# A gated delta rule's recurrence: one inverse product per block behind keys times state, instead of a second solve ahead of it

## The chip, the cores and the metric

The kernel runs on one core of a Trainium2 chip. The metric is the device time of one execution in microseconds; before the change it is 1047.45 us, the median of three runs (1047.32 to 1048.46).

## The reference

One layer of a hybrid block on 512 tokens of width 1024: a half-step SwiGLU feed-forward network, a token mixer, and a second feed-forward network, each behind an adaptive norm. The mixer has two groups of four heads: a gated delta rule (GDN) and latent attention (MLA). Only the delta rule's chunk recurrence is touched. With G the running sum of the log decays in a chunk, the reference computes per head and chunk:

```python
A = where(strict, beta[:, None] * (k @ k.T) * decay, 0)
M = A + eye(CHUNK)
rhs = concatenate([v * beta[:, None], k * (beta * exp(G))[:, None]], axis=-1)
u, wk = split(triangular_solve(M, rhs, lower=True, unit_diagonal=True))
# scan over chunks, state S of 128 x 128 per head:
v_new = u - wk @ S
o     = (q * exp(G)[:, None]) @ S + ((q @ k.T) * decay) @ v_new
S     = S * exp(G[-1]) + (k * exp(G[-1] - G)[:, None]).T @ v_new
```

Afterwards o is normalised per head, multiplied by a gate, and goes with the attention output through the output projection. Everything is float32.

## The kernel before

**Tiling.** Tokens are handled as four blocks p of 128 (the kernel's chunk for the recurrence), heads as four groups of 128 columns in a 128 x 512 tile. Dense products split both operands into a high and a low part and use three matmuls for each 128 x 128 weight tile (lines 267 to 269, `mm3`); the delta rule's own products are plain float32 matmuls of 128 x 128, which the trace shows as two matmul records each (x8 for the four heads).

**Order of the work.** The program is a set of Python generators that emit instructions; a `Side` holds generators and `step(n)` advances them n yields. A planner then orders each engine's queue by emission order among what it expects to be ready. In the mixer three sides matter: `chain` (the keys' norms, the matrix A, its blockwise inverse, the join of the inverse's 64-wide halves at lines 1639 to 1654, then the solves), `deltas` (queries, values), and `att` (attention). They are stepped between the dense products of the input projection. When those are done, a `while` loop at line 2066 steps them on; once attention is finished, `fill` holds `out_attended`: the attention half of the output projection, 32 steps of three 128 x 512 matmuls, each fourth followed by an update of xT on VectorE (line 2121), each eighth preceded by a weight load with its split (wh on ScalarE, line 193; wl on VectorE, line 198).

**The solves** (`solve`, line 1667): for each block, U (the transposed block inverse) times the scaled values gives u (line 1685), copied from PSUM by ScalarE; for blocks 1 to 3, decayed keys (kbg, a VectorE multiply at line 1678) times U gives w (line 1694), copied by ScalarE. The keys for the state update (kd) are scaled on VectorE as well (line 1681). Multiplies go through a helper and show as line 1232.

**The recurrence** (`recur`, line 1698), between lines 2080 and 2107: inside `matmuls_in_order` TensorE's instructions keep the order of emission, apart from those that are emitted by `loosely`. Each block yields twice. Before the first yield: w times S (line 1711), vn = u − that (VectorE, line 1713), S times its decay on GpSimd, q times S (line 1719) and its scaled copy (ScalarE, line 1721). After it: kd times vn (line 1726), the new S, qk times vn (line 1734), o. At each yield the loop puts in three steps of `fill` and two of `gated`. Block 0 has no state and needs no w.

**The gated output** (`gated_out`, line 1742) of a block is opened behind the block: square on ScalarE (hn, line 1772), sum (gs, line 1773) and ve (line 1748) on VectorE, a power on GpSimd (ry, line 179), a scaling on VectorE (on); then, at the next block's first yield and behind that yield's fill steps, four transposes on TensorE (line 1757) and the products with the gate (mf, mh, ml). They are in the kept order, not loose. After block 3 come `fill.step(4)` and the rest of the gated outputs, then the delta half of the output projection in two token halves (`out_half`), whose first half lies in `fill` as well.

**Buffers.** 128 x 512 tiles come from a pool of 56 (`slots`), some from a second pool of 12 (`late`); among the latter are all convolution outputs (`conv`, line 1431) and the gate z.

Of the kernel before, what the change touches and what calls it, by code (L numbers as in the profile page):

```python
# [14 lines left out]
AF = mybir.ActivationFunctionType  # L15
ALU = mybir.AluOpType
AX = mybir.AxisListType

P = 128
# [3 lines left out]
NB = NT // P  # L23
# [56 lines left out]
class Block:  # L80
# [1347 lines left out]
        self.table(d, d, AF.Exp)  # L1428
        return d

    def conv(self, p, ct):

        nc = self.nc
        a = self.slot(s="cv", late=True)
        wj = lambda j: self.cwT[:, 12 * j + ct:12 * j + ct + 1]
        nc.scalar.activation(a, p, AF.Copy, scale=wj(3))
        for d in range(1, 4):
            nc.vector.scalar_tensor_tensor(out=a[:, d:], in0=p[:, :NT - d], scalar=wj(3 - d), in1=a[:, d:], op0=ALU.mult,  # L1438
                                           op1=ALU.add)
        return a  # L1440
# [217 lines left out]
    def values(self, vT):  # L1658

        h4 = lambda x: x.rearrange("p (h d) -> p h d", h=4)  # L1660
        self.vb = []
        for p in range(NB):
            self.vb.append(self.slot(s="vb"))
            self.mul(h4(self.vb[p]), h4(self.token_major(vT, p)), self.bc(self.kn[:, 4 * p:4 * p + 4], 4))
            yield

    def solve(self, p):

        nc = self.nc
        h4 = lambda x: x.rearrange("p (h d) -> p h d", h=4)  # L1670
        hs = lambda h: slice(h * P, (h + 1) * P)
        c4 = slice(4 * p, 4 * p + 4)
        u = self.inv[p]
        vb = self.vb[p]
        kt = self.kt[p]
        if p > 0:
            kbg = self.slot(s="kbg")
            self.mul(h4(kbg), h4(kt), self.bc(self.eG[:, c4], 4))
        if p < NB - 1:
            self.kd[p] = self.slot(s="kd")  # L1680
            self.mul(h4(self.kd[p]), h4(kt), self.bc(self.kcd[:, c4], 4))
        yield
        pu = self.aux()
        for h in range(4):
            nc.tensor.matmul(pu[:, hs(h)], u[:, hs(h)], vb[:, hs(h)], start=True, stop=True)
        self.us[p] = self.slot(s="uu")
        nc.scalar.copy(self.us[p], pu)
        yield
        if p == 0:
            self.wk[p] = True  # L1690
            return
        pw = self.aux()
        for h in range(4):
            nc.tensor.matmul(pw[:, hs(h)], kbg[:, hs(h)], u[:, hs(h)], start=True, stop=True)
        self.wk[p] = self.slot(s="w")
        nc.scalar.copy(self.wk[p], pw)

    def recur(self, p):

        nc = self.nc  # L1700
        h4 = lambda x: x.rearrange("p (h d) -> p h d", h=4)
        hs = lambda h: slice(h * P, (h + 1) * P)
        S, last = self.S, p == NB - 1
        ts = slice(p * P, (p + 1) * P)
        o = self.slot(s="o")
        if S is None:
            vn = self.us[p]
        else:
            pw = self.aux()
            for h in range(4):  # L1710
                nc.tensor.matmul(pw[:, hs(h)], self.wk[p][:, hs(h)], S[:, hs(h)], start=True, stop=True)
            vn = self.slot(s="vn")
            nc.vector.tensor_tensor(out=vn, in0=self.us[p], in1=pw, op=ALU.subtract)
            if not last:
                sg = self.slot(s="Sg")
                self.mul(h4(sg), h4(S), self.bc(self.gl[:, 4 * p:4 * p + 4], 4), nc.gpsimd)
            pq = self.aux()
            for h in range(4):
                nc.tensor.matmul(pq[:, hs(h)], self.qT[h][:, ts], S[:, hs(h)], start=True, stop=True)
            for h in range(4):  # L1720
                nc.scalar.activation(o[:, hs(h)], pq[:, hs(h)], AF.Copy, scale=self.eG[:, 4 * p + h:4 * p + h + 1])
        yield
        if not last:
            pst = self.aux()
            for h in range(4):
                nc.tensor.matmul(pst[:, hs(h)], self.kd[p][:, hs(h)], vn[:, hs(h)], start=True, stop=True)
            self.S = self.slot(s="S")
            if S is None:
                nc.vector.tensor_copy(self.S, pst)
            else:  # L1730
                nc.vector.tensor_tensor(out=self.S, in0=sg, in1=pst, op=ALU.add)
        po = self.aux()
        for h in range(4):
            nc.tensor.matmul(po[:, hs(h)], self.qk[p][:, hs(h)], vn[:, hs(h)], start=True, stop=True)
        if S is None:
            nc.scalar.copy(o, po)
        else:
            nc.vector.tensor_tensor(out=o, in0=o, in1=po, op=ALU.add)
        self.o[p] = o
        yield  # L1740
# [238 lines left out]
    def mixer(self, nb):  # L1979
        nc, tc = self.nc, self.tc  # L1980
# [13 lines left out]

        def conv_done(ct0, dst):
            def f(i, p):
                dst.append(self.conv(p, ct0 + i))
            return f

        def silu(tiles):  # L2000
# [1 line left out]
                self.table(t, t, AF.Silu)  # L2002

        self.inv, self.ready64 = [None] * NB, [None] * NB
        self.kd, self.us, self.o, self.wk = ([None] * NB for _ in range(4))
        self.S = None

        def prepared():
# [31 lines left out]
        silu(vT)  # L2040
        deltas.add(self.values(vT))

        def solving():
            solves = Side(wide=2)
            solves.add(*(self.solve(p) for p in range(NB)))
            while solves.open or solves.todo:
                solves.step(2)
                yield

        chain.add(solving())  # L2050
# [12 lines left out]

        rest = Side(wide=3)
        rest.add(others())
        while self.wk[1] is None or deltas.open or deltas.todo:
            chain.step(2)
            deltas.step()
            rest.step(4)
            if not rest.open and not rest.todo:  # L2070
                fill.step(1)

        def loosely(side, n):
            with self.traced() as block:
                side.step(n)
            self.loose.update(i.name for i in block)
# [103 lines left out]
```

## Time and profile before

| what | value |
| --- | --- |
| median of three runs | 1047.45 us (1047.32 to 1048.46) |
| the profiled execution's own time | 1047.25 us |
| its span, first to last instruction | 1045.6 us |
| TensorE busy | 1029.0 us, 98% |
| VectorE busy | 682.6 us, 65% |
| ScalarE busy | 448.6 us, 43% |
| GpSimd busy | 48.2 us, 5% |
| granted TensorE clock | 0.999 |
| first solve (line 1685) starts | 626.1 us |
| last product of the recurrence (line 1734) starts | 661.1 us |

Times of instructions are from the span's start. A row of the timeline merges neighbours of one line: its start, its length, engine, line, operation, output and inputs by the program's names, shapes and count; a bracket at the end gives the idle time of the engine ahead of it and what ended it. Lengths on TensorE are modelled to the end of the pipeline, so neighbouring rows overlap, and the cost of a group in a stream is read from start to start.

### The profile page before, as it was taken

To read this page: it belongs to the slowest core of one execution; us is meant where nothing else is said; L and a number is where in the kernel's file an instruction comes from. 1 tells how busy PE (TensorE), PEld (TensorE's weight loads), DVE (VectorE), ACT (ScalarE), POOL (GpSimd) and SP (SyncE) were. 2 spreads that over 40 slices of the span, in tenths; PEclk is the share of its full clock that TensorE was granted. 3 is DMA by queue.
4 is the path that set the end of the run, shared out by engine and by line. 5 is a ranking of instruction groups with operands and counts; after the bars stand their busy time and mean duration, and the time that the engine had idled before them with its cause. 6 is when DMAs were issued, how large, how long until landed. Compare 5 with 4: busy or idle time off the path is not lost.

```text
span 1045.6 us, 16109 instructions
## 1 busy us (share of the span) xinstructions
PE 1029.0 (98%) x6379; PEld 882.2 (84%) x6379; DVE 682.6 (65%) x1251; ACT 448.6 (43%) x781; POOL 48.2 (5%) x113
## 2 busy tenths in 40 slices
PE   6999999999999999999999999999999999999998
PEld 4778878788887799888778779998999999999986
DVE  4488984333486636648878556788778778777633
ACT  4343222232222226749565464465345444344422
POOL 1000000000000011100010111310000000000000
PEclk9999999999999999999999999999999999999999
DMA  9989973323586439712212201173423334333222
GB/s 274 292 232 322 298 218 101 100 84 94 190 285 220 155 102 231 185 40 54 69 41 56 72 22 41 41 162 101 141 81 102 104 99 121 91 92 109 74 61 81
DMA packets 203689, 136.88 MB, mean 131 GB/s; under 512 B 13777, under 2 KB 186590, under 8 KB 203614
## 3 DMA queue, kind: packets, MB, share of 16 engines
q1 hardware_dynamic: 202318, 131.14, 42.6%
q0 software_dynamic: 1296, 4.72, 2.4%
q8 instruction: 50, 0.82, 0.3%
q14 instruction: 25, 0.20, 0.1%
HBM read 128.63 MB, written 2.49 MB: 125 GB/s over the span
## 4 chain that ended last, share of the span: by engine, by line
PE 90%; ACT 4%; DVE 4%; issue 1%; DMA 1%; POOL 0%; SPq 0%; POOLq 0%; ACTq 0%; DVEq 0%
PE pa L267 20%; PE pa L268 20%; PE pa L269 20%; PE pb L872 6%; PE pb L873 6%; PE pb L874 6%; PE pb L267 1%; PE pb L268 1%; PE pb L269 1%; PE pb L1909 1%; PE pb L418 1%; PE pb L1939 1%; PE pb L1494 1%; DVE cv L1438 1%; PE pb L1912 1%
## 5 line engine op out<-in xcount | busy, mean ns | idle before, releaser
L267 PE MATMUL pa<-hh,wh 128*128 128x512 f32 (+1 forms) x565 | 216.8, 384 | 0.4 <-ACT hh L465 0.4
L193 ACT CAST wh<-wr 128x1024 fp32r<-128x1024 f32 (+1 forms) x106 | 107.9, 1018 | 250.6 <-PE pa L268 177.8
L268 PE MATMUL pa<-hl,wh 128*128 128x512 f32 (+1 forms) x565 | 214.7, 380 | 0.5 <-DVE hl L457 0.3
L269 PE MATMUL pa<-hh,wl 128*128 128x512 f32 (+1 forms) x565 | 214.5, 380 | 0.0
L198 DVE TENSOR_TENSOR wl<-wr,wh 128x1024 fp32r<-128x1024 f32 (+1 forms) x97 | 114.2, 1178 | 104.0 <-ACT wh L193 101.6
L267 PE MATMUL pa<-ah,wh 128*128 128x512 f32 (+1 forms) x396 | 145.5, 368 | 0.6 <-DVE xT L899 0.4
L268 PE MATMUL pa<-al,wh 128*128 128x512 f32 (+1 forms) x396 | 144.5, 365 | 0.0
L269 PE MATMUL pa<-ah,wl 128*128 128x512 f32 (+1 forms) x396 | 143.5, 362 | 0.0
L267 PEld LDWEIGHTS pa<-hh,wh 128*128 128x128 f32 x565 | 106.4, 188 | 23.9 <-issue 3.3
L269 PEld LDWEIGHTS pa<-hh,wl 128*128 128x128 f32 x565 | 106.3, 188 | 20.6 <-issue 0.9
L268 PEld LDWEIGHTS pa<-hl,wh 128*128 128x128 f32 x565 | 106.5, 188 | 19.6 <-DVE hl L457 1.1
L269 PEld LDWEIGHTS pa<-ah,wl 128*128 128x128 f32 x396 | 74.8, 189 | 12.0
L267 PEld LDWEIGHTS pa<-ah,wh 128*128 128x128 f32 x396 | 75.2, 190 | 10.3 <-ACT wh L193 1.7
L268 PEld LDWEIGHTS pa<-al,wh 128*128 128x128 f32 x396 | 75.2, 190 | 7.2
L577 DVE SCALAR_TENSOR_TENSOR aa<-ar,sc,aa 128x512 f32<-128x512 f32 x98 | 72.9, 747 | 8.2 <-DMA ar<-in_w_ada 6.8
L872 PE MATMUL pb<-fh,wh 128*128 128x256 f32 x144 | 40.7, 283 | 0.0
L874 PE MATMUL pb<-fh,wl 128*128 128x256 f32 x144 | 40.7, 283 | 0.0
L874 PE MATMUL pb<-hh,wl 128*128 128x256 f32 x144 | 40.7, 283 | 0.0
L873 PE MATMUL pb<-fl,wh 128*128 128x256 f32 x144 | 40.7, 282 | 0.0
L873 PE MATMUL pb<-hl,wh 128*128 128x256 f32 x144 | 40.7, 282 | 0.0
L899 DVE SCALAR_TENSOR_TENSOR xT<-pa,mod,xT 128x512 f32<-128x512 f32 (+1 forms) x40 | 29.3, 735 | 17.3 <-PE pa L269 17.3
L872 PE MATMUL pb<-hh,wh 128*128 128x256 f32 x144 | 40.6, 282 | 0.0
(445 smaller groups left out, 2003.1 us busy)
## 6 DMA issues: line engine op xcount, KB each, us to landing
wr<-in_ffn_w_in SPq DMA_DIRECT2D x82, 512.0 KB, 3.9
ar<-in_w_ada SPq DMA_DIRECT2D x48, 512.0 KB, 6.1
wr<-in_ffn_w_out SPq DMA_DIRECT2D x34, 512.0 KB, 3.9
ar<-in_w_ada SPq DMA_DIRECT2D x48, 256.0 KB, 4.8
wr<-in_w_in SPq DMA_DIRECT2D x21, 512.0 KB, 4.3
wr<-in_ffn_w_out SPq DMA_DIRECT2D x17, 384.0 KB, 3.4
wl<-wr POOLq DMA_DIRECT2D x9, 512.0 KB, 6.1
wr<-in_w_out SPq DMA_DIRECT2D x8, 512.0 KB, 3.8
```

The source lines that it names most:

```text
L193: self.nc.scalar.copy(hi, raw)
L198: self.nc.vector.tensor_tensor(out=lo, in0=raw, in1=hi.bitcast(F32), op=ALU.subtract)
L267: mm(out, wh, xh, start=start, stop=False)
L268: mm(out, wh, xl, start=False, stop=False)
L269: mm(out, wl, xh, start=False, stop=stop)
L418: nc.tensor.matmul(pg[32 * q:32 * q + 32, :256], self.sc[:, kc:kc + 1].to_broadcast([P, 32]), a[:, kc], start=(e == 0), stop=(e == 1), til ...
L577: nc.vector.scalar_tensor_tensor(out=acc, in0=a, scalar=sc, in1=acc, op0=ALU.mult, op1=ALU.add)
L872: mm(out, wh, xh, start=start and k == 0, stop=False, **kw)
L873: mm(out, wh, xl, start=False, stop=False, **kw)
L874: mm(out, wl, xh, start=False, stop=stop and k == 3, **kw)
L899: nc.vector.scalar_tensor_tensor(out=self.xT[t][:, ts], in0=p[:, ts], scalar=gate[:, t:t + 1], in1=self.xT[t][:, ts], op0=ALU.mult, op1=AL ...
L1438: nc.vector.scalar_tensor_tensor(out=a[:, d:], in0=p[:, :NT - d], scalar=wj(3 - d), in1=a[:, d:], op0=ALU.mult, op1=ALU.add)
```

## The change

The second solve is left out by using linearity: with U the inverse, u − w S equals U applied to (scaled v − decayed (k S)). Per block, the keys themselves are multiplied with the state; VectorE forms r = exp(G) · (k S) − scaled v in four instructions of 128 columns; U times r is then one product, and ScalarE's copy with scale −1 gives vn. So `solve` is now called inside `recur`, behind a yield of its own; a block has three yields, with 1, 3 and 2 fill steps instead of 3 and 3 (block 0: two yields, 1 and 3). kbg, its multiply, its product and the copy of w are gone. kd's multiply overwrites the keys in place and is emitted with the values. As the transposed keys live to the last block, their convolution output comes from `slots`, not from `late`. The main loop ends when the first inverse exists, not when the solves of the first two blocks are emitted; the remaining steps of the join are then emitted loosely inside the recurrence.

```diff
-    def conv(self, p, ct):
+    def conv(self, p, ct, late=True):
...
-        a = self.slot(s="cv", late=True)
+        a = self.slot(s="cv", late=late)
...
             self.mul(h4(self.vb[p]), h4(self.token_major(vT, p)), self.bc(self.kn[:, 4 * p:4 * p + 4], 4))
+            if p < NB - 1:
+                self.mul(h4(self.kt[p]), h4(self.kt[p]), self.bc(self.kcd[:, 4 * p:4 * p + 4], 4))
             yield
...
-    def solve(self, p):
...
-        pw = self.aux()
-        for h in range(4):
-            nc.tensor.matmul(pw[:, hs(h)], kbg[:, hs(h)], u[:, hs(h)], start=True, stop=True)
-        self.wk[p] = self.slot(s="w")
-        nc.scalar.copy(self.wk[p], pw)
+    def solve(self, p, rhs, scale):
+        u = self.inv[p]
+        pu, vn = self.aux(), self.slot(s="vn")
+        for h in range(4):
+            hs = slice(h * P, (h + 1) * P)
+            nc.tensor.matmul(pu[:, hs], u[:, hs], rhs[:, hs], start=True, stop=True)
+        nc.scalar.activation(vn, pu, AF.Copy, scale=scale)
+        return vn
...
         if S is None:
-            vn = self.us[p]
+            vn = self.solve(p, self.vb[p], 1.0)
         else:
-            pw = self.aux()
+            eg = lambda h: self.eG[:, 4 * p + h:4 * p + h + 1]
+            pk, r = self.aux(), self.slot(s="r")
             for h in range(4):
-                nc.tensor.matmul(pw[:, hs(h)], self.wk[p][:, hs(h)], S[:, hs(h)], start=True, stop=True)
-            vn = self.slot(s="vn")
-            nc.vector.tensor_tensor(out=vn, in0=self.us[p], in1=pw, op=ALU.subtract)
+                nc.tensor.matmul(pk[:, hs(h)], kT[h][:, ts], S[:, hs(h)], start=True, stop=True)
+            for h in range(4):
+                nc.vector.scalar_tensor_tensor(out=r[:, hs(h)], in0=pk[:, hs(h)], scalar=eg(h), in1=self.vb[p][:, hs(h)],
+                                               op0=ALU.mult, op1=ALU.subtract)
...
+            yield
+            vn = self.solve(p, r, -1.0)
         yield
...
-        while self.wk[1] is None or deltas.open or deltas.todo:
+        while self.inv[0] is None or deltas.open or deltas.todo:
...
-                while self.wk[p] is None:
+                while self.inv[p] is None:
                     loosely(chain, 1)
-                for _ in self.recur(p):
+                for i, _ in enumerate(self.recur(p, kT)):
                     loosely(chain, 2)
                     loosely(rest, 4)
                     if not rest.open and not rest.todo:
-                        fill.step(3)
+                        fill.step((1, 3, 2)[i])
                     gated.step(2)
```

More of the change, by code (lines that the diff above doesn't have):

```diff
@@ L1664, in values, with recur @@
             self.mul(h4(self.vb[p]), h4(self.token_major(vT, p)), self.bc(self.kn[:, 4 * p:4 * p + 4], 4))
+            if p < NB - 1:
+                self.mul(h4(self.kt[p]), h4(self.kt[p]), self.bc(self.kcd[:, 4 * p:4 * p + 4], 4))
             yield
-    def solve(self, p):
+    def solve(self, p, rhs, scale):
         nc = self.nc
-        h4 = lambda x: x.rearrange("p (h d) -> p h d", h=4)
-        hs = lambda h: slice(h * P, (h + 1) * P)
-        c4 = slice(4 * p, 4 * p + 4)
         u = self.inv[p]
[L1674 to L1683, printed above, removed]
-        for h in range(4):
[L1685 to L1691, printed above, removed]
-        pw = self.aux()
-        for h in range(4):
-            nc.tensor.matmul(pw[:, hs(h)], kbg[:, hs(h)], u[:, hs(h)], start=True, stop=True)
-        self.wk[p] = self.slot(s="w")
-        nc.scalar.copy(self.wk[p], pw)
-    def recur(self, p):
+        pu, vn = self.aux(), self.slot(s="vn")
+        for h in range(4):
+            hs = slice(h * P, (h + 1) * P)
+            nc.tensor.matmul(pu[:, hs], u[:, hs], rhs[:, hs], start=True, stop=True)
+        nc.scalar.activation(vn, pu, AF.Copy, scale=scale)
+        return vn
+    def recur(self, p, kT):
         nc = self.nc
@@ L1720, in recur @@
             for h in range(4):
-                nc.scalar.activation(o[:, hs(h)], pq[:, hs(h)], AF.Copy, scale=self.eG[:, 4 * p + h:4 * p + h + 1])
+                nc.scalar.activation(o[:, hs(h)], pq[:, hs(h)], AF.Copy, scale=eg(h))
+            yield
+            vn = self.solve(p, r, -1.0)
         yield
@@ L1725, in recur @@
             for h in range(4):
-                nc.tensor.matmul(pst[:, hs(h)], self.kd[p][:, hs(h)], vn[:, hs(h)], start=True, stop=True)
+                nc.tensor.matmul(pst[:, hs(h)], self.kt[p][:, hs(h)], vn[:, hs(h)], start=True, stop=True)
             self.S = self.slot(s="S")
@@ L1996, in f @@
             def f(i, p):
-                dst.append(self.conv(p, ct0 + i))
+                dst.append(self.conv(p, ct0 + i, dst is not kT))
             return f
@@ L2004, in mixer @@
         self.inv, self.ready64 = [None] * NB, [None] * NB
-        self.kd, self.us, self.o, self.wk = ([None] * NB for _ in range(4))
+        self.o = [None] * NB
         self.S = None
@@ L2041, in mixer @@
         deltas.add(self.values(vT))
[L2043 to L2050, printed above, removed]
         self.dense_units(4, Rates(sides, (1, 0.75, 2)), 1, z_done)
```

## The prediction

> **What bounds the kernel now.** I read the page's totals first, then the busy table by stage, then the order of work on each engine around the delta rule. The totals and the chain that ended last (engine shares):
>
> ```profile
> span 1045.6 us, 16109 instructions
> PE 1029.0 (98%) x6379; PEld 882.2 (84%) x6379; DVE 682.6 (65%) x1251; ACT 448.6 (43%) x781; POOL 48.2 (5%) x113
> ...
> PE 90%; ACT 4%; DVE 4%; issue 1%; DMA 1%; POOL 0%; SPq 0%; POOLq 0%; ACTq 0%; DVEq 0%
> ```
>
> TensorE is idle for only 1045.6 − 1029.0 = 16.6 us of the whole span, so an edit can pay in two coins: TensorE work, or TensorE idle time. The busy table (columns: window, its length, then busy us of PE, PEld, DVE, ACT, POOL, granted clock, DMA share, GB/s) for the solves, the first block (first row) and the three recurring blocks:
>
> ```profile
> 626.10:639.10 13.00, 13.00 (x95) 12.09 (x95) 6.72 (x11) 5.28 (x10) 0.00 (x0) 1.00 0.14 42
> 639.10:647.30 8.20, 8.20 (x56) 7.29 (x55) 7.18 (x16) 3.87 (x10) 3.28 (x3) 1.00 0.22 64
> 647.30:655.40 8.10, 8.10 (x55) 7.30 (x54) 6.77 (x17) 3.31 (x9) 1.71 (x2) 1.00 0.18 50
> 655.40:661.20 5.80, 5.39 (x39) 4.64 (x37) 3.79 (x9) 2.04 (x7) 1.01 (x1) 1.00 0.08 23
> ```
>
> TensorE never waits here except for 0.41 us in the last block, at full granted clock (1.00), and VectorE is about 85% busy in the two middle blocks. One block in TensorE's order (columns: start, length, engine, line, tiles, count):
>
> ```profile
> 647.26 1.05 PE L1711 MATMUL pb<-S,w 128*128 128x128 f32 x8
> 648.15 1.06 PE L1719 MATMUL pb<-S,cv 128*128 128x128 f32 x8
> 648.96 0.48 PE L267 MATMUL pa<-mh,wh 128*128 128x512 f32 x1
> ...
> 649.74 0.39 PE L267 MATMUL pa<-mh,wh 128*128 128x512 f32 x1
> ...
> 651.11 0.60 PE L1757 MATMUL pb<-ident,on 128*128 128x128 f32 x4
> 651.54 1.06 PE L1726 MATMUL pb<-vn,kd 128*128 128x128 f32 x8
> 652.43 1.06 PE L1734 MATMUL pb<-vn,qk 128*128 128x128 f32 x8
> 653.25 0.48 PE L267 MATMUL pa<-mh,wh 128*128 128x512 f32 x1
> ...
> 655.42 1.05 PE L1711 MATMUL pb<-S,w 128*128 128x128 f32 x8
> ...
> 659.85 0.66 PE L1757 MATMUL pb<-ident,on 128*128 128x128 f32 x4 [0.41 <-DVE on L1232]
> ```
>
> From the starts: a product of four heads costs 0.89 us (0.82 where a fill step follows), the first fill step after one 0.78, each further one 0.69, the four transposes at L1757 0.43; a block is 655.42 − 647.26 = 8.16 us. The fill steps are what hides every hand-off.
>
> **TensorE work removed.** L1694 (keys times inverse) goes for three blocks:
>
> ```profile
> 627.97 1.06 PE L1694 MATMUL pb<-U,kbg 128*128 128x128 f32 x8
> 628.78 0.47 PE L267 MATMUL pa<-mh,wh 128*128 128x512 f32 x1
> ...
> 635.21 1.95 PE L1694 MATMUL pb<-U,kbg 128*128 128x128 f32 x16
> 636.91 0.47 PE L267 MATMUL pa<-mh,wh 128*128 128x512 f32 x1
> ```
>
> Three groups of 0.89 = **2.67 us**. The product with the state stays (keys instead of w), the four L1685 solves stay but move: from a stretch where nothing waited for them into the chain from state to state. The total of fill steps does not change.
>
> **Off TensorE.** Three kbg multiplies and three w copies vanish; vn's subtract becomes four 128-wide instructions (r); the kd multiply moves into the value preparation; the u copy becomes vn.
>
> ```profile
> 629.06 0.59 ACT L1696 COPY w<-pb 128x512 f32<-128x512 f32 x1 [0.31 <-PE pb L1694]
> ...
> 628.86 0.68 DVE L1232 TENSOR_TENSOR kbg<-ktk,eG 128x512 f32<-128x512 f32 x1
> 629.47 0.68 DVE L1232 TENSOR_TENSOR kd<-ktk,kcd 128x512 f32<-128x512 f32 x1
> ...
> 643.61 0.87 DVE L1763 SCALAR_TENSOR_TENSOR mf<-pb,cwT,z 128x128 f32<-128x128 f32 x3 [0.82 <-PE pb L1757]
> ```
>
> Those engines are no bound, so their 3 × 0.59 and 3 × 0.68 us pay nothing by themselves. The nearest row for r is mf, same operation, size and memory: 0.87 for three, so 0.27 per further one and **1.14 us for four**, against 0.68 for one subtract. [...]
>
> **The new chain, link by link.** Let T be the start of the keys-times-state product. TensorE order becomes: keys × S 0.89, q × S 0.82, one fill step 0.78, the transposes of the block before (they stay behind the first yield, whose fill drops from three steps to one), U × r, three fill steps, the two products with vn, two fill steps.
> - r: the product lands 1.05 after T, four instructions end at about T+2.23; U × r is reached at T+2.49 at the earliest. Covered by 0.26 us; with one weight subtract in front (wl, 1.22 below) it would be some 0.9 late.
> - vn: lands 1.06 after U × r starts, plus a 0.59 copy = 1.7; cover is 0.82 + 0.78 + 2 × 0.69 = 2.98. Hidden.
> - S: 1.06 + 0.69 (vn's subtract, same shape, in the rows below) after its product starts; cover 0.89 + 0.82 + 0.78 + 0.69 = 3.18. Hidden.
> - **The gated output** is what comes late. The rows of its chain (o, square, sum, ve, pow, scale) for one block:
>
> ```profile
> 655.07 0.68 DVE L1738 TENSOR_TENSOR o<-o,pb 128x512 f32<-128x512 f32 x1
> 655.67 0.74 DVE L2121 SCALAR_TENSOR_TENSOR xT<-pa,mod,xT 128x512 f32<-128x512 f32 x1
> 656.51 0.69 DVE L1713 TENSOR_TENSOR vn<-uu,pb 128x512 f32<-128x512 f32 x1
> 657.11 0.68 DVE L1773 TENSOR_REDUCE gs<-hn 128x4 f32<-128x512 f32 x1
> 657.82 0.16 DVE L1748 SCALAR_TENSOR_TENSOR ve<-gs,oe 128x4 f32<-128x4 f32 x1
> 659.11 0.69 DVE L1232 TENSOR_TENSOR on<-o,ry 128x512 f32<-128x512 f32 x1 [1.12 <-POOL ry L179]
> ```
>
> ```profile
> 655.84 0.63 ACT L1772 ACTIVATE hn<-o 128x512 f32<-128x512 f32 x1 [1.35 <-DVE o L1738]
> ```
>
> ```profile
> 658.07 1.01 POOL L179 TENSOR_TENSOR ry<-ve,mhalf 128x4 f32<-128x4 f32 x1 [7.87 <-DVE ve L1748]
> ```
>
> Start to start without queueing: product of qk to o 1.09, o to hn 0.77, hn to gs 0.67, gs to ve 0.71, ve to ry 0.25, ry to on 1.04, on to L1757 0.74: **5.27 us**. TensorE's work between those two points will be 0.82 + 0.78 + 0.69 + 0.89 + 0.82 + 0.78 = **4.78** (now it is 1.4 + 0.7 more, and the last block waited 0.41 all the same). So blocks two and three each wait some 0.49 at L1757. In block one o is an ACT copy and its cover a step longer, but r holds VectorE until T+2.23, so on can't start before and L1757 waits 2.23 + 0.74 − 2.49 = 0.48. The last gated output is emitted behind two steps and fill.step(4); some three of those four are now small ones of 0.69, because the main loop ends three to four steps earlier and the recurrence takes 22 steps instead of 24: cover 0.82 + 0.78 + 4 × 0.69 = 4.36, up to 5.05, against 5.27: 0.2 to 0.9, taken as 0.5. Sum 2 × 0.49 + 0.48 + 0.5 = **1.96**.
> - **VectorE traffic in that window.** xT (0.74) comes with every fourth step, and wl, 1.13 start to start, with every eighth:
>
> ```profile
> 651.50 1.22 DVE L198 TENSOR_TENSOR wl<-wr,wh 128x1024 fp32r<-128x1024 f32 x1
> 652.63 0.86 DVE L1763 SCALAR_TENSOR_TENSOR mf<-pb,cwT,z 128x128 f32<-128x128 f32 x3
> ```
>
> In the 18 steps of three blocks that is 4.5 × 0.74 + 2 × 1.13 = 5.6 us; the sensitive 4 us are some 0.45 of a block, so at most 2.5 us, at least 0. I take half, **1.2**.
> - **The start.** The first solve is pinned in TensorE's order once the first inverse exists, with three or four fewer free steps emitted before it. The join hands over between engines:
>
> ```profile
> 621.42 0.27 PE L1642 MATMUL pb<-U,Y 64*64 64x64 f32 x1
> ...
> 622.03 0.50 PE L269 MATMUL pa<-mh,wl 128*128 128x512 f32 x1
> 622.37 0.40 PE L267 MATMUL pa<-mh,wh 128*128 128x512 f32 x1
> ```
>
> ```profile
> 622.03 0.37 ACT L1654 COPY Y<-pb 64x256 f32<-64x256 f32 x1 [1.72 <-PE pb L1639]
> ```
>
> ```profile
> 622.14 0.42 DVE L1649 TENSOR_SCALAR U<-pb 64x256 f32<-64x256 f32 x1 [2.96 <-PE pb L1642]
> ```
>
> The copy of Y ends at 622.40 and U at 622.56, while TensorE's joined products end at about 622.03; fill steps stand in the gap today. Without them it is 0.4 to 0.5 once, bounds 0 and 1.0; I take **0.5**.
> - **kd early, keys in another pool.** The kd multiplies (0.68 each) now run while attention and its dense matmuls keep TensorE busy; the keys' convolution takes four buffers of the large pool until the last block instead of the late pool's. I cost both at 0. The bound is one multiply in a chain TensorE waits for, −0.7 to +0.7.
>
> **Sum** against the profiled execution (1047.25 us, span 1045.6, 0.2 below the median of 1047.45): −2.67 removed, −0.41 for today's wait at L1757, which is counted anew, +1.96 gated output, +1.2 traffic, +0.5 start = **+0.6**: 1047.8, so on the median some 1048. All terms at their lower ends (−3.08 + 1.46 + 0.2 − 0.7) give −2.1, at their upper ends (−3.08 + 1.46 + 0.9 + 2.5 + 1.0 + 0.7) +3.5.
>
> **Rivals.**
> A, *the work pays in full.* VectorE gets room: mf and ml no longer collide with S and o, as the transposes move ahead of U × r, and the pieces of the gated chain run at once or are overtaken by what I count as cover. Then −2.67 to −3.08: 1044.2 to 1044.6. For it: 98% TensorE and a recurrence with one wait. Against: the 5.27 against 4.78. [...]
> B, *VectorE's queue decides at L1757 (slower).* If the chain keeps the length that it has in today's last block, 659.85 − 652.43 = 7.42 instead of 5.27, each of blocks two and three waits 2.64 and the first and last perhaps 1.5 each: 8.3 + 0.5 − 3.08 = +5.7, near 1053. It decides from 5.2 us of waits in all. For it: wl, xT and four pieces of r in one in-order queue; against: S, o and mf no longer meet.
> C, *the schedule of attention shifts* through the four buffers and the early multiplies: ±1 us beside the sum, 1047 to 1049.
>
> **How the numbers follow.** 0.2% of 1047.45 is 2.1 us, about what a measurement of this kernel tells from nothing. Forecast 0.50 (0.43 within 0.2%, 0.03 faster, 0.04 slower); A 0.25, all faster; B 0.15, all slower; C 0.10 (0.05 same, 0.01 faster, 0.04 slower). Faster 0.29, same 0.48, slower 0.23. The forecast's own range is the sum's ends, 1045.1 to 1050.8; to hold 8 in 10 it reaches down to A: 1044.2 to 1050.8.
>
> **What would show it.** L1694 gone and 24 matmuls fewer; idle time on TensorE ahead of L1757 (releaser on) of 0.5 or more in each block, and next to none ahead of U × r, L1726 or keys × S; a short idle at the first solve. No idle at L1757 means A. Waits above 1.5 at L1757 in two blocks mean B. I am wrong in kind if the waits sit ahead of U × r (r late) or outside 600 to 700 us.

## The result, and the profile after

The changed kernel takes 1052.53 us (median of 21 executions, 1047.19 to 1055.24); the kernel before, beside it, 1047.56 us. The ratio is 1.0033, with a 95% interval of 1.0021 to 1.0044: some 0.3% slower, where the prediction said some 1048 us and no measurable change.

One thing is needed to understand that number: the executions of the changed kernel form two groups. In 9 of 21 the mean granted clock of TensorE is 0.999 or 1.0 and the median time is **1048.0 us**; in 12 of 21 the clock is 0.992 to 0.995 and the median is **1053.3 us**. Of the kernel before, 20 of 21 executions lie between 1046.99 and 1049.54 us, and one at 1052.71. So the sum of the prediction was met by one group, and the loss is in the other. The profiled execution (1052.53 us) is of the second group. From its page, the totals and the granted clock by fortieths of the span:

```profile
span 1050.8 us, 16053 instructions
PE 1030.6 (98%) x6355; PEld 884.0 (84%) x6355; DVE 682.1 (65%) x1257; ACT 447.0 (43%) x778; POOL 46.9 (4%) x113
...
PEclk9999999999999999999999989999999999999999
```

24 matmuls fewer (6379 to 6355), as announced, but TensorE is busy 1.6 us longer, not 2.67 us less. One digit of the clock row is an 8. The busy table of this kernel around that digit (window, length, busy us of PE, PEld, DVE, ACT and POOL, granted clock, DMA share, GB/s):

```profile
615.00:620.00 5.00, 4.79 (x86) 3.22 (x86) 2.93 (x9) 4.87 (x11) 0.00 (x0) 0.94 0.01 3
620.00:625.00 5.00, 4.50 (x40) 3.28 (x40) 1.17 (x2) 2.16 (x7) 0.00 (x0) 0.50 0.01 3
625.00:630.00 5.00, 5.00 (x40) 3.92 (x39) 0.83 (x2) 1.50 (x4) 0.00 (x0) 0.54 0.00 0
630.00:635.00 5.00, 5.00 (x38) 4.50 (x37) 3.75 (x6) 2.09 (x3) 0.11 (x1) 1.00 0.17 49
```

In windows of 0.4 us this trace has the clock at 0.50 in every one from 619.4 to 629.4 us and at 1.00 ahead of and behind that stretch, with 0.98 and 0.72 in the two windows where it changes. So a mean of 0.94 over five microseconds is 0.6 us at half rate; with 5.0 and 4.6 us in the next two windows, TensorE runs at half rate for **10.2 us**, from about 619.4 to 629.6, with its busy share at 90 to 100%. At half rate a product took about twice as long (the first solve, below: 2.07 us against 1.06), so this costs up to half of it, an estimated 5.1 us; this execution lies 4.5 us above the full-clock median of 1048.0. The mean clocks of 0.992 and 0.993 in eight of the twelve slower executions stand for more: if the lower clock is 0.50 in them too, twice the missing 0.7 to 0.8% of 1053 us is an estimated 15 to 17 us at half rate (the 0.994 of the profiled execution makes 12.6 in the same way); where it lies in them no trace shows. The first two windows in the kernel before, at 1.00:

```profile
615.00:620.00 5.00, 5.00 (x32) 3.23 (x33) 2.13 (x6) 3.78 (x10) 0.00 (x0) 1.00 0.02 5
620.00:625.00 5.00, 5.00 (x58) 3.23 (x59) 1.75 (x4) 2.19 (x5) 0.00 (x0) 1.00 0.00 0
```

The order of TensorE's work in the changed kernel at that place (start, length, line, tiles, count; a bracket gives the idle time ahead of a row):

```profile
612.76 1.23 PE L1956 MATMUL pb<-ident,on 128*128 128x128 f32 x8 [0.31 <-DVE on L1232]
613.91 0.95 PE L1597 MATMUL pb<-ti,at 32*32 32x32 f32 x48
...
615.46 1.79 PE L1608 MATMUL pb<-ti 32*32 32x32 f32 x64
617.17 0.63 PE L1618 MATMUL pb<-ident,U 64*64 64x64 f32 x8
...
623.14 0.36 PE L1642 MATMUL pb<-U,Y 64*64 64x64 f32 x1 [0.24 <-ACT Y L1654]
...
624.51 0.37 PE L1642 MATMUL pb<-U,Y 64*64 64x64 f32 x1 [0.25 <-ACT Y L1654]
...
625.55 2.07 PE L1676 MATMUL pb<-vb,U 128*128 128x128 f32 x8
```

The half rate begins among the 32- and 64-wide matmuls of the inverses, 6 us before the first solve (line 1676, 2.07 us long; L1694, the same shape and count, took 1.06 in the prediction's rows). Neither new product of the recurrence has run by then. The two idle times of 0.24 and 0.25 us are the prediction's "start".

The waits ahead of the gated output's transposes (now line 1743), the place that the prediction named, in the same view:

```profile
637.61 0.63 PE L1743 MATMUL pb<-ident,on 128*128 128x128 f32 x4 [0.44 <-DVE on L1232]
...
648.68 0.63 PE L1743 MATMUL pb<-ident,on 128*128 128x128 f32 x4 [1.82 <-DVE on L1232]
...
658.30 0.66 PE L1743 MATMUL pb<-ident,on 128*128 128x128 f32 x4 [0.37 <-DVE on L1232]
...
667.04 0.66 PE L1743 MATMUL pb<-ident,on 128*128 128x128 f32 x4 [0.82 <-DVE on L1232]
```

Their sum is 3.45 us. From 613 us to the end of the recurrence the view has no other row with a bracket than these four and the two of the join, so none ahead of U × r, of the products with vn or of keys × S. Why the second wait is four times the first, in VectorE's order of this kernel:

```profile
643.03 0.69 DVE L1724 TENSOR_TENSOR o<-o,pb 128x512 f32<-128x512 f32 x1
643.73 0.75 DVE L2099 SCALAR_TENSOR_TENSOR xT<-pa,mod,xT 128x512 f32<-128x512 f32 x1
644.58 1.23 DVE L198 TENSOR_TENSOR wl<-wr,wh 128x1024 fp32r<-128x1024 f32 x1
645.72 0.68 DVE L1759 TENSOR_REDUCE gs<-hn 128x4 f32<-128x512 f32 x1
...
647.85 0.69 DVE L1232 TENSOR_TENSOR on<-o,ry 128x512 f32<-128x512 f32 x1 [0.34 <-POOL ry L179]
```

An xT update and a weight's wl stand between o and gs. From o to on it is 647.85 − 643.03 = 4.82 us, where the prediction's links without queueing make 0.77 + 0.67 + 0.71 + 0.25 + 1.04 = 3.44: 1.38 us more, which with the predicted 0.49 gives 1.87 for the 1.82 seen.

### The profile page after: what moved, and what is told of

It reads as the page before. It is cut to its first block, busy times and chain, and to the rows that moved or that the text cites. A ratio compares the mean times of both kernels' runs of the same rounds, so it can differ in the third digit from the quotient of the medians.

```text
span 1050.8 us, 16053 instructions
## 1 busy us (share of the span) xinstructions
PE 1030.6 (98%) x6355; PEld 884.0 (84%) x6355; DVE 682.1 (65%) x1257; ACT 447.0 (43%) x778; POOL 46.9 (4%) x113
## 3 DMA queue, kind: packets, MB, share of 16 engines
HBM read 128.63 MB, written 2.49 MB: 125 GB/s over the span
## 4 chain that ended last, share of the span: by engine, by line
PE 92%; DVE 3%; ACT 2%; DMA 1%; issue 1%; POOL 0%; SPq 0%; POOLq 0%; DVEq 0%; ACTq 0%
PE pa L267 21%; PE pa L268 21%; PE pa L269 21%; PE pb L873 6%; PE pb L872 6%; PE pb L874 6%; PE pb L267 1%; PE pb L269 1%; PE pb L268 1%; PE pb L418 1%; PE pb L1494 1%; PE pb L1895 1%; DMA xt<-in_x 1%; PE pb L1898 0%; PE pb L1925 0%
```

## The experiments

Two things had to be settled: what halves the clock, and whether the sum's terms are right at full clock. Theory **D** (density): the shorter main loop leaves too few dense 128 x 512 matmuls among the small ones of the inverse and join, and TensorE's clock falls there. Rival **R**: the new recurrence with its waits brings it about. Rival **N**: it is chance and has nothing to do with the kernel. The number that was taken to go with D is how many dense matmuls ran in the 6.8 us ahead of the drop; the last paragraph of this section says how far it carries. The busy table of the tile pa alone (the accumulator of the dense matmuls; columns as above without POOL), first of the kernel before:

```profile
612.80:616.20 3.40, 1.64 (x4) 0.56 (x3) 0.00 (x0) 0.00 (x0) 1.00 0.48 151
616.20:619.60 3.40, 2.61 (x9) 1.53 (x9) 0.75 (x1) 0.00 (x0) 1.00 0.02 5
```

and the same windows, and the next three, of the changed kernel:

```profile
612.80:616.20 3.40, 0.73 (x2) 0.30 (x2) 0.00 (x0) 0.00 (x0) 1.00 0.34 116
616.20:619.60 3.40, 1.26 (x4) 0.52 (x4) 0.00 (x0) 0.00 (x0) 0.97 0.00 0
619.60:623.00 3.40, 2.04 (x4) 1.12 (x4) 0.75 (x1) 0.00 (x0) 0.50 0.02 5
623.00:626.40 3.40, 0.00 (x0) 0.00 (x0) 0.00 (x0) 0.00 (x0) 0.50 0.00 0
626.40:629.80 3.40, 1.18 (x2) 0.50 (x2) 0.00 (x0) 0.00 (x0) 0.53 0.00 0
```

13 dense matmuls before, 6 after. (Time at half rate from these clocks: 2 × 3.4 × (0.03 + 0.50 + 0.50 + 0.47) = 10.2 us again.)

**1. The main loop of the changed kernel runs on until all four inverses exist.**

```diff
-        while self.inv[0] is None or deltas.open or deltas.todo:
+        while self.inv[NB - 1] is None or deltas.open or deltas.todo:
```

> The changed kernel with one edit: the main loop runs until the last block's inverse exists, not the first, so some three more of the free fill steps (three dense 128x512 matmuls each) are emitted beside the join. Theory D (thin stretch): the granted clock falls to 0.5 for about 10 us in the join (from 620 us on in the changed kernel's profile) because there the join's 32- and 64-wide matmuls have too few dense matmuls between them; a halved clock over 10.2 us costs some 5 us. D expects the half clock in few executions or none, and a time near 1047.5 with the waits ahead of the gated transposes left as they are. Theory R (recurrence): the new chain's waits draw the clock down; then this edit changes nothing, most executions stay at 1052 to 1055. Theory N (chance of the chip at that hour): same share of slow-clock executions in every kernel, the one before too.

Measured: 1053.47 us against 1047.82, ratio 1.0046 (1.0032 to 1.0060); clock 0.994 or 0.995 in 4 of 6 executions, 0.998 in the other two. D had expected the halved clock to go; in the profiled execution it only came later. The tile pa in this kernel:

```profile
623.00:626.40 3.40, 0.82 (x4) 0.35 (x2) 1.21 (x2) 0.00 (x0) 1.00 0.02 5
626.40:629.80 3.40, 0.00 (x0) 0.00 (x0) 0.00 (x0) 0.00 (x0) 0.67 0.38 113
```

The longer loop brings the fill steps that go with it earlier, and the end of the join stands without any. So the length of the loop is not the cause by itself; which small matmuls stand alone may still be. From 612.8 to 619.6 us this kernel has 12 dense matmuls, nearly as many as the kernel before, and from 619.6 to 626.4, ahead of the drop, 12 again: the count that went with D does not tell this run from one at full clock.

**2. The gated output of the changed kernel is stepped behind the solve instead of ahead of it** (all three of its steps at a block's second yield).

```diff
-                    gated.step(2)
+                    if i == 1:
+                        gated.step(3)
```

> The changed kernel with one edit: the gated output's scaling and transposes are emitted behind the second yield's three fill steps (behind U x r), not behind the first yield's one step. My prediction's step says the waits ahead of the transposes, 0.44 + 1.82 + 0.37 us in blocks one to three in the profile, are a chain that comes late by what stands ahead of it on VectorE; with 0.89 + 3 x 0.7 = 3 us more cover they should be 0, and only the last one (0.82) stay: -2.6 us in executions at full clock, so near 1045.4. The rival (r is late): a wait appears ahead of U x r instead, and the gain is under 1 us. D expects the half clock in the join to stay as often as in the changed kernel (13 of 21), since the join is untouched; R expects it to go.

(The 13 of 21 in that text is a miscount; it is 12 of 21.) Measured: 1050.73 us, ratio 1.0018 (1.0003 to 1.0034). Four of twelve executions at full clock, 1045.70 to 1046.82, middle 1046.1; eight at 0.992 to 0.995, 1049.73 to 1053.21. The profiled execution is a full-clock one, and its rows with idle time on TensorE from 613 to 676 us are:

```profile
621.72 0.27 PE L1642 MATMUL pb<-U,Y 64*64 64x64 f32 x1 [0.41 <-ACT Y L1654]
622.75 0.27 PE L1642 MATMUL pb<-U,Y 64*64 64x64 f32 x1 [0.35 <-ACT Y L1654]
639.91 1.16 PE L1694 MATMUL pb<-S,cv 128*128 128x128 f32 x8 [0.18 <-DVE S L1717]
661.01 0.65 PE L1743 MATMUL pb<-ident,on 128*128 128x128 f32 x4 [1.56 <-DVE on L1232]
```

The three waits inside the recurrence are gone and the last has grown: 1.74 us instead of 3.45, 1.71 less, and the full-clock times differ by 1.9 (1048.0 to 1046.1). The waits cost about what the trace says. The clock falls about as often as in the changed kernel, with almost no waits left in the recurrence: this is against R.

**3. Two fill steps per round of the main loop instead of one, in the changed kernel.**

```diff
             if not rest.open and not rest.todo:
-                fill.step(1)
+                fill.step(2)
```

> The changed kernel with one edit: the main loop emits two fill steps per round once attention is done, so about 14 instead of 7 of the 32 stand beside the inverse and the join; the recurrence's own fill then reaches into the delta half of the output projection. D expects no half clock in the join at all and a time near 1047.5 or a little below (the short waits of the join, 0.24 + 0.25 us, are filled as well). R and N expect the half clock as often as before.

Measured: 1046.78 us (1045.83 to 1047.71), ratio 0.9988 (0.9979 to 0.9996), clock 0.999 or 1.0 in all 11 executions. The tile pa:

```profile
612.80:616.20 3.40, 0.96 (x3) 0.49 (x3) 0.00 (x0) 0.00 (x0) 1.00 0.04 11
616.20:619.60 3.40, 2.34 (x9) 1.64 (x10) 0.75 (x1) 0.00 (x0) 1.00 0.02 5
```

and its waits:

```profile
637.27 0.63 PE L1743 MATMUL pb<-ident,on 128*128 128x128 f32 x4 [1.16 <-DVE on L1232]
647.69 0.63 PE L1743 MATMUL pb<-ident,on 128*128 128x128 f32 x4 [1.19 <-DVE on L1232]
657.31 0.66 PE L1743 MATMUL pb<-ident,on 128*128 128x128 f32 x4 [0.36 <-DVE on L1232]
```

12 dense matmuls instead of 6, no lowered clock in any execution, and 2.71 us of waits left in the untouched recurrence. R falls by this. The two waits of the join are gone too.

**4. The kernel before, with a fill step only in every second round of its main loop.**

```diff
             if not rest.open and not rest.todo:
-                fill.step(1)
+                thin += 1
+                fill.step(thin % 2)
```

> The kernel before with one edit the other way: the main loop emits a fill step only every second round, about 5 instead of 10 beside the inverse and the join; the rest comes later, in the same total. No work is added or removed. D expects the half clock to appear in the join of the kernel before, in a good part of the executions, with 1051 to 1055 there, and 1047 to 1048.5 in the others. R and N expect no change against the kernel before, 1047.5.

Measured: 1050.19 us, ratio 1.0022 (1.0013 to 1.0030), and full clock in all 11 executions: D missed as it was stated. The tile pa shows why:

```profile
612.80:616.20 3.40, 1.69 (x5) 0.57 (x4) 0.00 (x0) 0.00 (x0) 1.00 0.49 159
616.20:619.60 3.40, 2.85 (x10) 1.72 (x10) 0.61 (x1) 0.00 (x0) 1.00 0.00 0
...
626.40:629.80 3.40, 0.00 (x0) 0.00 (x0) 0.00 (x0) 0.00 (x0) 1.00 0.00 0
629.80:633.20 3.40, 0.00 (x0) 0.00 (x0) 0.00 (x0) 0.00 (x0) 1.00 0.55 159
```

The planner filled the inverses as before (15 in the same windows), and the thinning fell behind them, where 6.8 us of solves without one dense matmul keep the full clock. So it is not dense matmuls as such: here the clock stayed at 1.00 over 128-wide products alone, and what is left to test is the stretch of the 32- and 64-wide ones. The 2.4 us of loss (1050.19 against 1047.82) lie near the added waits: 0.73 us in the join and 0.63 and 1.84 ahead of L1757, 3.20 against 0.41 before.

**5. The kernel before, with the first eight fill steps of the main loop held back.**

```diff
             if not rest.open and not rest.todo:
-                fill.step(1)
+                held += 1
+                fill.step(int(held > 8))
```

> The kernel before with the first eight fill steps of the main loop held back, so only two steps (six dense 128x512 matmuls) stand beside the 32- and 64-wide matmuls of the inverse and the join, as in the changed kernel; no work is added or removed, and the new recurrence is not in it. Theory D, made sharper by the last runs (thinning only behind the inverse left the clock alone): what draws the clock to 0.5 is some 7 us of TensorE work in 32- and 64-wide tiles with two dense steps or fewer. D expects a granted clock of 0.992 to 0.996 in most executions, and times of 1052 to 1057 there (half clock over 7 to 10 us costs 3.4 to 5, some us of idle join on top). Rival (the changed recurrence or its order is needed for it): clock 0.999 to 1.0 in all, the time only some 2 to 5 us up by the join's waits.

Measured: 1050.32 us against 1047.59, ratio 1.0021 (1.0009 to 1.0032); clock 1.0 in 7 of 9 executions, 0.996 and 0.998 in two (1052.55 and 1051.82, the slowest). D had expected most, and missed. The kernel before, run beside it, has a clock of 0.996 to 0.998 in 4 of 26 executions (1049.74 to 1051.05 us), so 2 of 9 are not told from the kernel before. The tile pa has 4 and 5 dense matmuls in the two windows, and experiment 9, without any fill step in the loop, has 5 and 4: these do not come from the main loop. The run decides nothing.

**6. Edits 2 and 3 together.**

> The changed kernel with both edits: two fill steps per round of the main loop, and the gated output's scaling and transposes behind the second yield. The two-step kernel alone has waits of 1.16 + 1.19 + 0.36 us ahead of the transposes at 1046.78; if these are the price of the place, they go: 1044.1 to 1045, with the clock full in all executions. If VectorE's queue is the limit and the wait only moves on (to r, S or the last gated output, where the gated edit alone shows 0.18 and 1.56), 1046 to 1047.

Measured: **1043.86 us** (1043.40 to 1044.16), ratio **0.9959** (0.9947 to 0.9971), clock 0.999 or 1.0 in all five executions. This version beats both kernels. The one row with idle time on TensorE from 613 to 676 us:

```profile
643.73 1.16 PE L1694 MATMUL pb<-S,cv 128*128 128x128 f32 x8 [0.18 <-DVE S L1717]
```

Against the changed kernel at full clock: 3.45 − 0.18 us of waits and the join's 0.41 + 0.35 (of experiment 2) make 4.0; measured 1048.0 − 1043.86 = 4.1. The changed kernel itself was not run beside this one.

**7. The kernel before without the product that goes** (w is a copy of the decayed keys; the product of keys and inverse is left out, and so the recurrence computes with other numbers).

```diff
-        pw = self.aux()
-        for h in range(4):
-            nc.tensor.matmul(pw[:, hs(h)], kbg[:, hs(h)], u[:, hs(h)], start=True, stop=True)
         self.wk[p] = self.slot(s="w")
-        nc.scalar.copy(self.wk[p], pw)
+        nc.scalar.copy(self.wk[p], kbg)
```

> The kernel before without the product of decayed keys and inverse (12 head products in three blocks): w is a copy of the decayed keys, so the delta rule's result is another; the copies, the product with the state and the order stay. My prediction prices the removed product at 3 x 0.89 = 2.67 us, all of it TensorE time that nothing hides: 1044.9 against 1047.6. Rival: TensorE's time in this stretch is not the bound and the wait moves to the gated transposes (0.41 us wait in the last block grows): 1045.5 to 1047.

Measured: 1046.12 us, ratio 0.9984 (0.9975 to 0.9992): 1.5 us gained, by the interval 0.8 to 2.6, not 2.67. Its rows with idle time on TensorE from 613 to 676 us (the transposes are line 1754 here):

```profile
643.33 0.63 PE L1754 MATMUL pb<-ident,on 128*128 128x128 f32 x4 [1.05 <-DVE on L1232]
660.22 0.66 PE L1754 MATMUL pb<-ident,on 128*128 128x128 f32 x4 [0.44 <-DVE on L1232]
```

1.49 us where the kernel before has 0.41: 2.67 − 1.08 = 1.59. The profiled execution is a late one (1047.66 us), but its 1.8 us of delay stand ahead of this stage: from the last L1576 to the start of the recurrence's last product it takes 63.98 us (596.73 to 660.71), the kernel before 65.43 (594.92 to 660.35). The removed product was itself cover for the gated output's chain. The prediction had taken the whole 2.67 to be gained; the run gives 1.5.

**8. The kernel before with the side moves alone:** the keys' convolution in the large pool, kd scaled with the values (its multiply in the solve goes).

```diff
-        a = self.slot(s="cv", late=True)
+        a = self.slot(s="cv", late=late)
...
             self.mul(h4(self.vb[p]), h4(self.token_major(vT, p)), self.bc(self.kn[:, 4 * p:4 * p + 4], 4))
+            if p < NB - 1:
+                self.kd[p] = self.slot(s="kd")
+                self.mul(h4(self.kd[p]), h4(self.kt[p]), self.bc(self.kcd[:, 4 * p:4 * p + 4], 4))
             yield
```

> The kernel before with only the two side edits of the change: the keys' convolution takes buffers of the large pool, and the multiplies for kd are emitted with the values. The prediction costs both at 0, with bounds of 0.7 either way: 1047.0 to 1048.3 at full clock. If these edits are what moves the four early fill steps ahead of the inverse (in the changed kernel they run at 609.5 to 612.3, before the 32-wide matmuls), the thin stretch and the half clock appear here as well, 1051 to 1053 in a good part; if not, the clock stays full.

Measured: 1046.63 us, ratio 0.9989 (0.9981 to 0.9998): −1.0 us, full clock in all but one of 11 executions (0.997). Not the cause of the lowered clock by itself, and worth about a microsecond (by the interval 0.2 to 2.0) that the prediction had at zero. Its idle time in the recurrence is the same as before (0.44 ahead of the last transposes, against 0.41), so where the microsecond lies the trace doesn't say.

**9. The kernel before without any fill step in its main loop.**

```diff
             if not rest.open and not rest.todo:
-                fill.step(1)
+                pass
```

> The kernel before with no fill step in the main loop at all: the 32- and 64-wide matmuls of the inverse and the join run with no dense matmul of the output projection between them, and its 32 steps all come later. Nothing is added or removed. Holding back eight of ten steps left 9 to 10 dense matmuls in the 6.8 us after 612.8 us and gave a lower clock in 2 of 9 executions; the changed kernel has 6 there and a half clock in 12 of 21. Theory D: with 0 there the half clock comes in most executions (granted clock 0.990 to 0.996), 1053 to 1060. Rival R (something of the changed recurrence is needed): clock 0.999 to 1.0, the time up by the join's waits alone, 1050 to 1054.

Measured: 1054.26 us against 1047.48, ratio 1.0065 (1.0052 to 1.0079), clock 0.995 or 0.996 in all five executions. The tile pa:

```profile
616.20:619.60 3.40, 1.73 (x4) 0.67 (x4) 0.00 (x0) 0.00 (x0) 1.00 0.16 56
619.60:623.00 3.40, 0.00 (x0) 0.00 (x0) 0.00 (x0) 0.00 (x0) 1.00 0.02 5
623.00:626.40 3.40, 0.00 (x0) 0.00 (x0) 0.00 (x0) 0.00 (x0) 0.56 0.00 0
626.40:629.80 3.40, 0.00 (x0) 0.00 (x0) 0.00 (x0) 0.00 (x0) 0.50 0.00 0
629.80:633.20 3.40, 0.00 (x0) 0.00 (x0) 0.00 (x0) 0.00 (x0) 0.94 0.00 0
```

The kernel before, with its own recurrence, falls to half rate for 2 × 3.4 × (0.44 + 0.50 + 0.06) = 6.8 us in the profiled execution, once the join's 64-wide matmuls stand alone, and the mean clock is as low in all five. The change is not needed for it, so R falls a second time, and 5 of 5 beside 0 of 9 for the kernel before is not N's chance. Ahead of this drop TensorE was also idle more (busy 1.62 and 1.46 of 2 us from 618 to 620 and from 620 to 622 us), so this run alone does not part small tiles from idle time; the changed kernel, busy 4.79 of 5 us as its drop began, does.

**10. The changed kernel with three dense matmuls whose result nobody reads, per round of the main loop after attention.** They add 21 matmuls (6376 against 6355).

```diff
             if not rest.open and not rest.todo:
                 fill.step(1)
+                for _ in range(3):
+                    nc.tensor.matmul(unread, self.mixed[4][0][:, :P], self.mixed[5][0], start=True, stop=True)
```

> The changed kernel with three unread dense 128x512 matmuls (two of the attention outputs multiplied into a bank that nobody reads) added in each round of the main loop once attention is done: some 21 matmuls of 0.23 us, 4.8 us of TensorE work more, part of it in waits of the join. The real fill steps, the recurrence and the waits ahead of the gated transposes stay. D expects the half clock to go: granted clock 0.999 to 1.0 in nearly all executions, and one group of times at 1048.0 + 4 to 4.8 = 1052 to 1053 instead of two. R expects the half clock as often as in the changed kernel (12 of 21): two groups, about 1052 and 1057.

Measured: 1053.07 us (1052.05 to 1054.13), clock 0.999 or 1.0 in all five executions; one group. The tile pa, with the unread ones in it:

```profile
612.80:616.20 3.40, 1.06 (x5) 0.59 (x4) 0.00 (x0) 0.00 (x0) 1.00 0.49 159
616.20:619.60 3.40, 1.14 (x4) 0.39 (x4) 0.00 (x0) 0.00 (x0) 1.00 0.00 0
619.60:623.00 3.40, 3.13 (x13) 2.28 (x14) 0.75 (x1) 0.00 (x0) 1.00 0.02 5
```

The work is the same and more, the waits of the recurrence are unchanged (0.44, 1.84, 0.36 and 0.79 us), and the drop and the two waits of the join are gone. The price of 5.1 us over the full-clock group (1048.0) is near that of 21 dense matmuls at 0.69 / 3 = 0.23 us, 4.8; as a remedy it gains nothing, where experiment 3 costs no work. It is no pure addition: of 26 dense matmuls in its join 12 are unread and 14 real, where the changed kernel has 6, so the planner dealt the real ones out anew. And the changed kernel was not run beside it: 0 of 5 stands against 12 of 21 from an earlier series, while in experiments 1 to 3, which ran side by side, it is 6 of 6 and 8 of 12 against 0 of 11.

**11. The same kernel once more.**

> The same kernel with the unread matmuls once more, for one profile beside the timed runs: D expects no stretch with a granted clock below 1.0 between 600 and 700 us, and at least 10 dense matmuls in each 6.8 us between 610 and 626 us.

Measured: 1052.05 us at clock 0.999, waits 0.43, 1.83, 0.37 and 0.82 us: with the drop or without it, the waits at the transposes are the same.

**What the runs together say.** D as first stated (the loop's length, or dense matmuls as such) failed in 1, 4 and 5; what stands is narrower: where the 32- and 64-wide matmuls of the inverse and the join ran with few dense ones between them (0 to 7 in the table below), the mean clock was under 0.999 in 2 of 9 to all of the executions, and where a profile caught it the clock was 0.50.

The count in fixed windows does not order the runs (experiment 1 has 12 and a low clock in 6 of 6, experiment 6 has 9 and 0 of 5), since the same time is another place of the program in another kernel. Counted afterwards from the last L1618 of the inverse to the last L1642 of the join, the dense matmuls of the profiled execution, and the executions with a mean clock under 0.999, are:

| kernel | dense matmuls in the join | clock under 0.999 |
| --- | --- | --- |
| before | 18 | 5 of the 64 run beside the experiments |
| experiments 3 and 6 | 24 | 0 of 11, 0 of 5 |
| experiment 4 | 15 | 0 of 11 |
| experiments 7 and 8 | 18, 19 | 1 of 11 each |
| experiments 10 and 11 | 26 | 0 of 6 |
| changed kernel | 6 | 12 of 21 |
| experiment 1 | 7 | 6 of 6 |
| experiment 2 | 6 | 8 of 12 |
| experiment 5 | 6 | 2 of 9 |
| experiment 9 | 0 | 5 of 5 |

This parts the two sets, but it was chosen after the results and is no rule: in the profiled execution of the changed kernel the drop begins at 619.4 us, where the join has yet to start, with 5 dense matmuls in the 6.8 us ahead of it. A mean clock also does not say where the clock fell: the page of experiment 1's profiled execution has an 8 in the clock row's first fortieth as well (0 to 26.3 us), far from the join. A rival that no run was made for is idle time in the join, which most of the kernels with a low clock have. The traces speak against it: the drop of the changed kernel comes 3.5 us ahead of the join's first wait, and experiment 4 with 0.73 us of waits there, and the profiled execution of experiment 5 with 1.44, keep the full clock. Not settled: which count of what activity decides, and why the planner issues four fill steps at 609.5 to 612.3 us, ahead of the inverse, in the changed kernel.

## Why the prediction was right and wrong

- **The sum, at full clock: right, in part because errors cancel.** 1048.0 us measured, some 1048 predicted. The terms, one by one:
- *Work removed, −2.67.* 24 matmuls fewer, right; but alone it pays 1.5 (experiment 7, interval 0.8 to 2.6), since the chain behind it gets less cover. The prediction's own count of that cover, 4.78 against 5.27, holds this loss in the next term, so nothing was counted twice.
- *Waits at the gated output's transposes, 1.96 + 1.2 = 3.16.* Measured 3.45: 0.44 for 0.48, 1.82 and 0.37 for 0.49 each, 0.82 for 0.5, the excess of 1.38 in the second being the xT and wl that the traffic term had named. Place and releaser were right and the size was near; that the 1.2 came close is partly luck, as it was the middle of a range of 0 to 2.5. Rival A (no waits, 1044.2 to 1044.6) and rival B (waits of 2.64) fall.
- *The start, 0.5.* At full clock 0.41 + 0.35 = 0.76 (experiment 2), within the bounds of 0 to 1.0.
- *U × r, vn and S covered.* No wait there, right. Four pieces of r take 1.12 us in the trace, 1.14 predicted. The prediction's own order puts the transposes (0.43) ahead of U × r, so by its rows U × r comes at T+2.92, not T+2.49: the cover was larger than it counted.
- *kd early and the keys' other pool, 0.* Mis-sized: −1.0 us (experiment 8), where the interval of 0.2 to 2.0 doesn't exclude the bound of 0.7; rival C had named these two edits with ±1 us. With it and the measured waits the sum is −2.67 − 0.41 + 3.45 + 0.76 − 1.0 = +0.1, and +0.4 was measured (1048.0 against 1047.56).
- **The step that failed** is the term "The start". It had the cause in its hands, "with three or four fewer free steps emitted before it", though by the traces only two steps fewer ran ahead of the first solve (21 dense matmuls of the output projection instead of 27), and four of the seven left ran in one piece before 612.3 us: from the 48 products of L1597 to the first solve there were 9 dense matmuls instead of 26. It priced this as idle time at one hand-off alone ("I take 0.5", bounds 0 and 1.0) and put any change of the clock at nothing, without a reason. The 1.00 that the prediction read ("at full granted clock") is of the kernel before, and its rows begin at 626.10 us, behind the inverse and most of the join. The runs showed in its place that the fill steps between the small matmuls did a second job: with two of them per round the clock was 0.999 or 1.0 in 11 executions of 11 (experiment 3), with one it was under 0.999 in 12 of 21. With so few of them 10.2 us ran at half rate in the profiled execution, and the 12 of 21 executions with a lowered clock have a median 5.3 us above the others, which no rival had. Rival B's number (near 1053) came out for this slower group by luck: the mechanism was not B's.
- What the changed kernel's trace shows of the clock: in windows of 1 us it is 1.00 or 0.50, with other values only where it changes, and 0.50 stands in two places, the 10.2 us above and the end of the span from about 1049.5 us, 2 us behind TensorE's last work. In experiment 9 the lowered stretch is 6.8 us long. Idle time of TensorE does not explain the drop at 619.4 us: in the changed kernel the largest from 612 to 619 us was 0.31 us, and TensorE was busy 4.79 us of five as the clock fell. What sets those lengths, and why one program falls in some executions and not in others, no run here tests.

## What to carry to other kernels

Before thinning the filler of a stretch of small matmuls, ask what the filler does beside hiding hand-offs: look at the granted clock there, and count the wide matmuls in it before and after. When TensorE is near 100% busy, an edit that removes its work may pay only part, since the removed work was cover for another chain: here some 1.5 of 2.67 us. Two lines of emission order (two fill steps per round, the gated output behind the solve) turned a change of +0.3% into one of −0.4%, so a restructured recurrence should be judged with its filler dealt out anew.

## What the hardware showed that was not expected

TensorE's granted clock is halved while TensorE is busy by the record: for 10.2 us in the profiled execution of the changed kernel (busy 4.50 to 5.00 us of each five) and for 6.8 us in that of experiment 9 (busy 1.70 to 2.00 us of each two from 624 to 630 us), each time behind 32- and 64-wide matmuls with few dense ones among them. 6.8 us of 128-wide float32 products without any dense matmul did not bring it about (experiment 4), and with 21 unread dense matmuls it was absent in six executions of six (experiments 10 and 11). One and the same program falls in some of its executions and not in others (12 of 21), and a single profile can show either.
